# Full-array chunk products, paired chunk matrices and more block-product tiles in a hybrid attention and RWKV-7 block

## The chip, the core and the metric

The kernel runs on one core of a Trainium2 chip. The metric is the device time of one execution in microseconds. Times are the median of several executions; the profile is of one more execution of the same program.

## What is computed

A decoder block for 512 tokens of 1024 channels, all in float32. A normed input goes through one projection; its columns feed sparse attention (an indexer picks 128 keys per query) and an RWKV-7 recurrence of 8 heads of 64 channels. Both are gated, added, projected and added to the input. Then follows a gated feed-forward layer of 2816 hidden channels.

```python
# the recurrence, per token and head
def step(state, inp):
    r_t, d_t, k_t, v_t, kk_t, b_t = inp
    s_a = jnp.einsum('bhvk,bhk->bhv', state, -kk_t)
    state = state * d_t[:, :, None, :] + s_a[..., None] * b_t[:, :, None, :] \
        + v_t[..., None] * k_t[:, :, None, :]
    return state, jnp.einsum('bhvk,bhk->bhv', state, r_t)
...
h = h + merged @ w_out[l]
hn = _rms_norm(h, ffn_norm[l])
gate, up = _split(hn @ w_gate_up[l], (FFN_HIDDEN, FFN_HIDDEN))
h = h + (jax.nn.silu(gate) * up) @ w_down[l]
```

## The kernel before

**Order of the work.** TensorE's instructions run in the order in which the program emits them. The program is a set of generators (`Streams`, line 96) with ranks: `steps` 0, `inverses` and attention 1, `matrices` and `prepare` 2, norms 3, and the dense products (`products`) last, at 9. A generator yields a number of microseconds, or the name of a signal, and is resumed when that time has passed by a count of TensorE's work; meanwhile the next in rank is emitted. So dense products fill every gap of the recurrence. The instructions of the other engines are ordered when the program is built, by a simulation of their times, and then run in that fixed order on each engine.

**Dense products.** Weights come as chunks of 512 KB (`chunk`, line 232): loaded into `w_raw` (2 buffers), rounded by ScalarE into `w_hi`, the rest by GpSimd or VectorE into `w_lo` (3 buffers each). `dense_t` (line 255) runs three passes for each of eight blocks of 128 channels: high by high, high by low, low by high. PSUM has three tags: `d` and `c` with three banks, `i` with two.

**The recurrence** goes in 8 chunks of 64 tokens, two (`e` = 0, 1) in each of four tiles `t` of 128 tokens.
- `matrices` (line 754): for each chunk two groups `g` of heads (rows 0 to 63 and 64 to 127 of `KB` and `KR`), four products each into one `d` bank; VectorE masks the bank into `am[g]` (line 771) and adds the identity (line 775), ScalarE copies a part to `l16` (line 776). After each group the generator yields 0.5.
- `inverses` (line 781): triangular inverses by f16 products in the `i` banks.
- `chunk_values` (line 735): transposes the values of a tile and copies the halves to `ve[0:64]` and `vo[64:128]` (lines 740, 741); the other halves are filled later by the chunk's solution (line 898).
- `steps` (line 853), for each chunk: the first product of `am` with `vu` into `psz` (line 877); the product with the state, for which `KR` is the stationary side (line 881); the right side `B` (line 884); its product with the inverse (line 897) and `vu`'s other half (line 898); the state's growth (line 904) and the new state (lines 911 to 916); the last product of `am` with `vu` (line 920), which adds to `psz`, and the chunk's output `y` (line 921).

With `br` the half of the rows that the chunk's solution takes and `er` the other, a 64-row, 64-column operand puts a matmul into a quarter of the array, a 128-row, 64-column one into half of it:

```python
for h in range(H):
    cs = slice(h * 64, h * 64 + 64)
    r = br if h else slice(0, 128)
    mm(psz[r, cs], am[h % 2][er, h // 2, r], vu[er, cs], start=h == 0, stop=False, **go)
```

**Gate and up** (line 1135): 22 tiles of 128 hidden columns, for gate and up each. A plain tile is two `dense_t` of 24 passes over 512 tokens. The others take the 2x2 block scheme with 7 products: from the raw chunks `wg` and `wu` VectorE makes four sums `s1` to `s4` (lines 1149 to 1152), ScalarE and VectorE split seven 128x512 sides into high and low (lines 1155, 1156), TensorE runs `product` (line 1127) seven times, 12 passes of 256 tokens each, and VectorE adds the results (lines 1176, 1179, 1182, 1188, 1192) and multiplies (lines 1195, 1196); four banks are taken for each such tile. The token sides are made once (`seven_sides`, line 1221). From j = 2 on every third tile is plain. `wu` has three buffers (`fx`), the sums share eight (`uc`) with other tiles.

Of the kernel before, what the change touches and what calls it, by code (L numbers as in the profile page):

```python
# [82 lines left out]
for _n, _c in _PARS:  # L83
# [5 lines left out]
L = dict(norm=3.0, normed=1.3, score=0.6, pick=0.15, rms=9.0, sums=4.0, attn=(1.3, 1.1, 1.0, 1.0), attn_new=0.7, attn_out=2.0, sig=0.3,  # L89
         prep=5.0, oper=6.0, bonus=9.0, mat=0.5, mats=2.8, inv_u=4.2, inv_t=1.4, inv_r=1.4, inv_n=0.9, inv_e=1.8,  # L90
         inv=1.8, vals=0.6, st_b=1.0, st_u=1.36, st_m=1.4, hn_b=4.55, hn_n=6.55, hn_g=2.0)
# [36 lines left out]
def hybrid_block(ctx: ExitStack, tc: tile.TileContext, x, first, rows, consts, lora, rel_bias, stream, out):  # L128
    nc = tc.nc
# [9 lines left out]
    def bank(tag, dt=F32, name=None):  # L139
        n = {"d": 3, "i": 2, "c": 3}[tag]  # L140
        return pp.tile([128, 512], dt, name=name or "ps_" + tag, tag=tag, bufs=n)

    def unit(name, dt=F32):

        tag = "ua" if name in UA else "uc"
        return sp.tile([128, 512], dt, name=name, tag=tag, bufs=UNITS[tag])
# [14 lines left out]
    def mm(o, w, r, **kw):  # L161
        nc.tensor.matmul(o, w, r, **kw)  # L162
        n = 1
        for d in r.shape[1:]:
            n *= d
        st.now += max(n * 4 / 2400, 0.107) if r.dtype == F32 else max(n / 2400, 0.03)

    def flip(o, src, idn):
        nc.tensor.transpose(o, src, idn)  # L169
        st.now += 0.11  # L170
# [47 lines left out]
    def cst(name):  # L218
        o, e = CONST_AT[name]
        return con[:, o:e]  # L220
# [27 lines left out]
    def w_tile(n, eng=None):  # L248

        r = []  # L250
        for _ in range(n // 128):
            r += chunk(1024 // n, n, eng)
        return r
# [481 lines left out]
    def chunk_values(t):  # L735
        ps = bank("c")
        for p in range(4):
            flip(ps[:, p * 128:p * 128 + 128], zv[:, p, t * 128:t * 128 + 128], ident)
        ve, vo = unit("vu"), unit("vu")
        nc.scalar.activation(ve[0:64], ps[0:64], AF.Copy)  # L740
        nc.scalar.activation(vo[64:128], ps[64:128], AF.Copy)
        return ve, vo
# [11 lines left out]
    def matrices():  # L754
        yield "prep"
        for t in range(NT):
            if t > 1:
                yield f"inv{t - 2}"
                yield f"step{t - 2}"
            l16 = l16s[t % 2]  # L760
            for e in range(2):
                c = 2 * t + e
                am = [unit("am").rearrange("q (h t) -> q h t", h=4) for _ in range(2)]
                br = BLK[e]
                for g in range(2):
                    ps = bank("d").rearrange("q (h t) -> q h t", h=4)
                    for j in range(4):
                        o = g * 64
                        mm(ps[:, j], zz["KB"][j][o:o + 64, t, 2 * e:2 * e + 2], zz["KR"][j][o:o + 64, t, 2 * e:2 * e + 2],
                           start=True, stop=True)  # L770
                    nc.vector.tensor_mul(am[g], ps, cst("mask_a")[:, None, 64 - 64 * e:192 - 64 * e]
                                         .to_broadcast([128, 4, 128]))
                    hs = slice(g, H, 2)
                    lt = am[g][br, :, br]
                    nc.vector.tensor_add(lt, lt, ident[br, None, br].to_broadcast([64, 4, 64]))
                    nc.scalar.activation(l16[br, hs, br], lt, AF.Copy)
                    yield L["mat"]
                A[t, e] = am
            st.signal(f"mat{t}", L["mats"])

# [72 lines left out]
    def steps():  # L853
        M, M2 = None, mst[0]
        yield "zv"
        for t in range(NT):
            yield f"mat{t}"
            vus = chunk_values(t)
            y = unit("ytok")
            for e in range(2):  # L860
                c, vu, am = 2 * t + e, vus[e], A[t, e]

                br, er = BLK[e], BLK[1 - e]
                if c < 7:
                    kbs, kbt = unit("kbs"), unit("kbt")
                    p3 = lambda q: q.rearrange("q (p s) -> q p s", p=4)
                    nc.gpsimd.tensor_mul(p3(kbs), zz["KB_"][:, :, t, 2 * e:2 * e + 2].rearrange("q p a b -> q p (a b)"),
                                         PC[:, c, :, None].to_broadcast([128, 4, 128]))
                if e == 0:
                    yield L["vals"]  # L870
                psz = bank("c")

                go = dict(skip_group_check=True)
                for h in range(H):
                    cs = slice(h * 64, h * 64 + 64)
                    r = br if h else slice(0, 128)
                    mm(psz[r, cs], am[h % 2][er, h // 2, r], vu[er, cs], start=h == 0, stop=False, **go)
                if c:
                    yield f"state{c}"
                    for p in range(4):  # L880
                        mm(psz[:, p * 128:p * 128 + 128], zz["KR"][p][:, t, 2 * e:2 * e + 2], M[:, p], start=False,
                           stop=False, **go)
                B = unit("bmat")
                nc.vector.tensor_copy(B[br], psz[br])
                if c < 7:
                    pst = bank("c")
                    for p in range(4):
                        cs = slice(p * 128, p * 128 + 128)
                        flip(pst[:, cs], kbs[:, cs], ident)
                    nc.scalar.activation(kbt, pst, AF.Copy)  # L890
                if e == 0:
                    yield f"inv{t}"
                yield L["st_b"]
                psu = bank("c")
                for h in range(H):
                    cs = slice(h * 64, h * 64 + 64)
                    mm(psu[br, cs], U32s[t][br, cs], B[br, cs], start=True, stop=True)
                nc.vector.tensor_scalar(vu[br], psu[br], -1.0, None, op0=OP.mult)
                yield L["st_u"]
                if c < 7:  # L900
                    psg = bank("c")
                    for h in range(H):
                        p, o, cs = h // 2, (h % 2) * 64, slice(h * 64, h * 64 + 64)
                        mm(psg[o:o + 64, p * 64:p * 64 + 64], kbt[:, cs], vu[:, cs], start=True, stop=True)
                    g3 = psg[:, 0:256].rearrange("q (p v) -> q p v", p=4)
                    if c:
                        mp = bp.tile([128, 256], F32, name="mp", tag="mp", bufs=1).rearrange("q (p v) -> q p v", p=4)
                    for o in (0, 64):
                        q = slice(o, o + 64)
                        if c:  # L910
                            nc.gpsimd.tensor_mul(mp[q], M[q, :, q], PC[q, c, :, None].to_broadcast([64, 4, 64]))
                            nc.vector.tensor_add(M2[q, :, q], g3[q], mp[q])
                        else:
                            nc.vector.tensor_copy(M2[q, :, q], g3[q])
                    M, M2 = M2, mst[(c + 1) % 2]
                    st.signal(f"state{c + 1}", L["st_m"])
                for h in range(H):
                    cs = slice(h * 64, h * 64 + 64)
                    r = slice(0, 128) if h else br
                    mm(psz[er, cs], am[h % 2][r, h // 2, er], vu[r, cs], start=False, stop=h == 7, **go)  # L920
                nc.scalar.activation(y[er], psz[er], AF.Copy)
            st.signal(f"step{t}")
            st.add(3, head_norm(t, y))
# [64 lines left out]
    def products(wt, w2):  # L988
# [116 lines left out]
        def next_bank():  # L1105
            turn[0] += 1
            return bank(tags[(turn[0] - 1) % 8])

        def plain(j, ps, pu):
            g = unit("gsig")  # L1110
            nc.scalar.activation(g, ps, AF.Silu)
            nc.vector.tensor_mul(up_rows(j), pu, g)
# [20 lines left out]
                mm(ps, lo[:, ks], xh, start=False, stop=k == 3, skip_group_check=True)  # L1133

        for j in range(2, NF):
            if j % 3 == 2:
                ps, pu = next_bank(), next_bank()
                yield from dense_t(ps, w_tile(128, nc.vector), slice(0, 128), hn)
                yield from dense_t(pu, w_tile(128, nc.vector), slice(0, 128), hn)
                plain(j, ps, pu)  # L1140
                continue
# [56 lines left out]
        for g in range(2):  # L1198
            cs = slice(g * 512, g * 512 + 512)
            pss = [bank(tag) for tag in (("c", "c", "c", "i") if g == 0 else ("d", "d", "d", "i"))]  # L1200
            for k0 in range(0, NF, 2):
# [8 lines left out]
                for t, k in [(t, k) for t in range(NT) for k in range(2)] if last else [(t, k) for k in range(2)  # L1210
                                                                                   for t in range(NT)]:
                    j, ts = k0 + k, slice(t * 128, t * 128 + 128)
# [129 lines left out]
```

## Time and profile before

| | us |
|---|---|
| median of 3 executions | 909.22 |
| lowest, highest | 909.14, 909.89 |
| the profiled execution | 909.72 |
| its span, first to last instruction | 907.90 |
| outside the span | 1.82 |

The profile lists every instruction of the core with start and length. A matmul's length includes its latency, so rows overlap and the start of the next one tells what a pass costs. One f32 matmul of the program stands as two passes. The chunk stage lies from about 276 to 450 us of the span, gate and up from about 570 to 784.

### The profile page before, as it was taken

What the parts mean: (1) busy time and instruction counts of PE and PEld (TensorE: products, weight loads), DVE (VectorE), ACT (ScalarE), POOL (GpSimd) and SP (SyncE); (2) the same over time, 40 slices, a digit from 0 to 9 for tenths busy, and PEclk for the clock granted to TensorE, in tenths of its full rate; (3) what the DMA queues carried; (4) which work ended last, traced back from release to release, by engine and by line L of the source; (5) the groups of instructions that cost most, each with busy time, mean ns of one, the idle gap of its engine ahead of it and who ended that gap; (6) DMA issues with size and microseconds to landing.
All of it is one profiled execution on the core that took longest, in us unless ns stands there. A gap on an engine that the chain in (4) does not pass through costs nothing.

```text
span 907.9 us, 14949 instructions
## 1 busy us (share of the span) xinstructions
PE 891.5 (98%) x6018; PEld 775.3 (85%) x6018; DVE 572.6 (63%) x1064; ACT 394.0 (43%) x665; POOL 296.6 (33%) x216
## 2 busy tenths in 40 slices
PE   6999999999999999999999999999999999999998
PEld 5988898888687788887888998899999999988886
DVE  5279997786886457666435428777677667433433
ACT  5464586554643333334243234534344434434431
POOL 6477873221473444354146422000000000323321
PEclk9999999999999999999999999999999999999999
DMA  6331333111131210011433323232224132332431
GB/s 241 82 95 49 94 119 94 47 47 36 48 93 47 71 47 25 25 48 46 143 91 93 95 92 117 74 136 96 91 93 140 57 106 70 93 114 89 147 93 47
DMA packets 24182, 77.88 MB, mean 86 GB/s; under 512 B 2869, under 2 KB 4366, under 8 KB 24112
## 3 DMA queue, kind: packets, MB, share of 16 engines
q1 hardware_dynamic: 20688, 72.49, 25.6%
q10 hardware_dynamic: 3424, 4.43, 1.8%
q8 instruction: 47, 0.77, 0.3%
q14 instruction: 23, 0.19, 0.1%
HBM read 74.53 MB, written 2.38 MB: 85 GB/s over the span
## 4 chain that ended last, share of the span: by engine, by line
PE 84%; DVE 9%; POOL 2%; issue 2%; ACT 2%; DMA 1%; ACTq 0%; POOLq 0%; DVEq 0%
PE ps_d L162 48%; PE ps_c L162 19%; PE ps_i L162 14%; PE ps_c L169 2%; DVE score L447 2%; DVE max L446 2%; POOL w_lo L243 1%; DVE kr L716 1%; DVE sg L681 1%; DVE qs L470 1%; PE ps_i L169 0%; DVE score L427 0%; DMA grow<-in_rows_dram 0%; POOL bb L710 0%; POOL ag L719 0%
## 5 line engine op out<-in xcount | busy, mean ns | idle before, releaser
L243 POOL TENSOR_TENSOR w_lo<-w_raw,w_hi 128x1024 fp32r<-128x1024 f32 (+1 forms) x67 | 158.5, 2368 | 421.3 <-ACT w_hi L239 414.1
L239 ACT ACTIVATE w_hi<-w_raw 128x1024 fp32r<-128x1024 f32 x103 | 108.7, 1056 | 129.5 <-PE ps_d L162 93.9
L162 PE MATMUL ps_d<-xnl,w_hi 128*128 128x512 f32 (+2 forms) x360 | 141.4, 393 | 0.0
L162 PE MATMUL ps_d<-xnh,w_lo 128*128 128x512 f32 (+2 forms) x360 | 140.6, 390 | 0.4 <-POOL w_lo L243 0.4
L162 PE MATMUL ps_d<-xnh,w_hi 128*128 128x512 f32 (+2 forms) x360 | 140.7, 391 | 0.0
L162 PEld LDWEIGHTS ps_d<-xnh,w_lo 128*128 128x128 f32 x360 | 68.2, 189 | 12.2 <-issue 1.2
L162 PEld LDWEIGHTS ps_d<-xnl,w_hi 128*128 128x128 f32 x360 | 68.2, 190 | 11.8 <-issue 2.1
L162 PEld LDWEIGHTS ps_d<-xnh,w_hi 128*128 128x128 f32 x360 | 68.3, 190 | 10.7 <-issue 1.2
L1207 DVE TENSOR_TENSOR us<-u,us 128x512 fp32r<-128x512 f32 x44 | 36.7, 835 | 64.2 <-ACT us L1206 64.2
L243 DVE TENSOR_TENSOR w_lo<-w_raw,w_hi 128x1024 fp32r<-128x1024 f32 x38 | 49.2, 1296 | 18.9 <-ACT w_hi L239 18.3
L1206 ACT ACTIVATE us<-u 128x512 fp32r<-128x512 f32 x44 | 27.8, 632 | 67.4 <-PE ps_i L162 67.2
L162 PE MATMUL ps_d<-hnl,w_hi 128*128 128x256 f32 (+1 forms) x144 | 46.0, 319 | 0.4 <-DVE hnl L338 0.4
L162 PE MATMUL ps_d<-hnh,w_hi 128*128 128x256 f32 (+1 forms) x144 | 45.9, 319 | 0.0
L162 PE MATMUL ps_d<-hnh,w_lo 128*128 128x256 f32 (+1 forms) x144 | 45.9, 319 | 0.0
L162 PE MATMUL ps_c<-w_hi,us 128*128 128x512 f32 x132 | 44.1, 389 | 0.0
L162 PE MATMUL ps_d<-w_hi,us 128*128 128x512 f32 x132 | 44.1, 389 | 0.0
L1156 DVE TENSOR_TENSOR w_lo<-s,w_hi 128x512 fp32r<-128x512 f32 x39 | 26.1, 685 | 22.2 <-ACT w_hi L1155 22.2
L162 PE MATMUL ps_d<-w_hi,mh 128*128 128x256 f32 x120 | 34.0, 284 | 0.0
L162 PE MATMUL ps_d<-w_hi,ml 128*128 128x256 f32 x120 | 34.0, 283 | 0.0
L162 PE MATMUL ps_d<-w_lo,mh 128*128 128x256 f32 x120 | 34.0, 283 | 0.0
L162 PE MATMUL ps_i<-w_hi,us 128*128 128x512 f32 x88 | 33.9, 389 | 0.0
L584 ACT ACTIVATE lg<-lg,mx,qrs 128x128 f32<-128x128 f32 (+3 forms) x32 | 20.9, 652 | 24.9 <-DVE mx L583 24.9
(381 smaller groups left out, 2429.4 us busy)
## 6 DMA issues: line engine op xcount, KB each, us to landing
w_raw<-in_stream_dram SPq DMA_DIRECT2D x116, 512.0 KB, 3.5
wu_raw<-in_stream_dram SPq DMA_DIRECT2D x13, 512.0 KB, 4.3
xa<-in_x_dram SPq DMA_DIRECT2D x4, 512.0 KB, 5.8
ht<-in_x_dram ACTq DMA_DIRECT2D x8, 256.0 KB, 3.9
out_dram<-ht SPq DMA_DIRECT2D x8, 256.0 KB, 2.1
toep<-bias_table ACTq DMA_DIRECT2D x8, 128.0 KB, 3.5
gain<-in_rows_dram ACTq DMA_DIRECT2D x2, 256.0 KB, 4.1
con<-in_consts_dram SPq DMA_DIRECT2D x1, 321.0 KB, 7.0
```

The source lines that it names most:

```text
L162: nc.tensor.matmul(o, w, r, **kw)
L169: nc.tensor.transpose(o, src, idn)
L239: nc.scalar.activation(hi, raw, AF.Copy)
L243: eng.tensor_sub(lo[:, o:o + n_], raw[:, o:o + n_], hi[:, o:o + n_])
L446: nc.vector.max(m8, sc)
L447: nc.vector.match_replace(sc, m8, sc, TAKEN)
L470: nc.vector.scalar_tensor_tensor(lo[b, h], src[a], gain[a], hi[a, h], op0=OP.mult, op1=OP.subtract)
L584: nc.scalar.activation(lg, lg, AF.Exp, scale=scale, bias=mx[:, 2:3], accum_out=den[:, h:h + 1])
L681: nc.vector.tensor_tensor_scan(cum, seg, cum, 0.0, op0=OP.mult, op1=OP.add)
L1156: nc.vector.tensor_sub(l, w, h)
L1206: nc.scalar.activation(s[:, 0], up[k0 // 2][:, k], AF.Copy)
L1207: nc.vector.tensor_sub(s[:, 1], up[k0 // 2][:, k], s[:, 0])
```

## The change

Four places.
- `chunk_values`: two memsets by GpSimd zero the halves of `ve` and `vo` that are not yet filled, so that all 128 rows can be read.
- `steps`, first product: all heads use all 128 rows and give all 128 outputs. `steps`, last product: all heads use only the rows `br` and give the outputs `er`. What the last product added from the rows `er` now comes with the first.
- `matrices`: one yield of twice the time behind both groups, in place of one behind each.
- Gate and up: every sixth tile is plain in place of every third. Of j = 2 to 21 the plain ones were 2, 5, 8, 11, 14, 17 and 20 and are 2, 8, 14 and 20; 5, 11 and 17 are now block products.

```diff
--- before.py
+++ after.py
@@ -737,6 +737,9 @@
         ve, vo = unit("vu"), unit("vu")
+
+        nc.gpsimd.memset(ve[64:128], 0.0)
+        nc.gpsimd.memset(vo[0:64], 0.0)
         nc.scalar.activation(ve[0:64], ps[0:64], AF.Copy)
         nc.scalar.activation(vo[64:128], ps[64:128], AF.Copy)
         return ve, vo
@@ -774,7 +777,7 @@
                     nc.scalar.activation(l16[br, hs, br], lt, AF.Copy)
-                    yield L["mat"]
+                yield 2 * L["mat"]
                 A[t, e] = am
@@ -873,8 +876,7 @@
                     cs = slice(h * 64, h * 64 + 64)
-                    r = br if h else slice(0, 128)
-                    mm(psz[r, cs], am[h % 2][er, h // 2, r], vu[er, cs], start=h == 0, stop=False, **go)
+                    mm(psz[:, cs], am[h % 2][:, h // 2], vu[:, cs], start=h == 0, stop=False, **go)
@@ -916,8 +918,7 @@
                     cs = slice(h * 64, h * 64 + 64)
-                    r = slice(0, 128) if h else br
-                    mm(psz[er, cs], am[h % 2][r, h // 2, er], vu[r, cs], start=False, stop=h == 7, **go)
+                    mm(psz[er, cs], am[h % 2][br, h // 2, er], vu[br, cs], start=False, stop=h == 7, **go)
@@ -1133,7 +1134,7 @@
         for j in range(2, NF):
-            if j % 3 == 2:
+            if j % 6 == 2:
                 ps, pu = next_bank(), next_bank()
```

## Rows read from the trace of the kernel before

**Rows 1.** The page's engine table: busy us (share of the span), instructions.

```profile
PE 891.5 (98%) x6018; PEld 775.3 (85%) x6018; DVE 572.6 (63%) x1064; ACT 394.0 (43%) x665; POOL 296.6 (33%) x216
```

**Rows 2.** Waits of TensorE: engine, line, releaser: us in all, times, longest.

```profile
PE ps_c L162 <- DMA grow<-in_rows_dram: 5.0, 1, 5.0
PE ps_i L169 <- DVE xnl L338: 2.4, 3, 1.0
```

**Rows 3.** Tile `yr`: count, ns least/median/most, first and last start (us), shapes.

```profile
L162 PE MATMUL ps_d<-yr,w_hi x64: 389/389/389, 479.3 to 500.7; 128*128 128x512 f32 x64
...
L1059 DVE TENSOR_TENSOR yr<-zv,yr x4: 684/684/694, 469.0 to 470.8; 128x512 fp32r<-128x512 f32 x4
```

**Rows 4.** Timeline, TensorE: start (us), length (us), engine, line, operation, shapes, count [idle].

```profile
284.02 1.16 PE L162 MATMUL ps_d<-kr,kb 64*128 64x128 f32 x8
285.10 0.50 PE L162 MATMUL ps_d<-xnh,w_lo 128*128 128x512 f32 x1
...
286.00 1.16 PE L162 MATMUL ps_d<-kr,kb 64*128 64x128 f32 x8
```

**Rows 5.** Timeline, TensorE, from three stretches: attention, and two of a chunk.

```profile
206.67 1.00 PE L162 MATMUL ps_i<-vt,pt 128*128 128x64 f32 x8
...
321.49 1.14 PE L162 MATMUL ps_c<-bmat,u 64*64 64x64 f32 x16
322.57 0.50 PE L162 MATMUL ps_d<-xnh,w_lo 128*128 128x512 f32 x1
...
333.87 1.28 PE L162 MATMUL ps_c<-vu,am 64*64 64x64 f32 x16
```

**Rows 6.** Timeline, TensorE, from an even chunk's end into an odd one.

```profile
324.45 0.69 PE L162 MATMUL ps_c<-vu,kbt 128*64 128x64 f32 x16
325.06 2.60 PE L162 MATMUL ps_c<-vu,am 64*64 64x64 f32 x32
327.59 1.16 PE L162 MATMUL ps_c<-state,kr 128*128 128x128 f32 x8
328.59 0.60 PE L169 MATMUL ps_c<-fst,kbs 128*128 128x128 f32 x4
```

**Rows 7.** Timeline, TensorE, the start of an even chunk.

```profile
335.90 1.16 PE L162 MATMUL ps_d<-kr,kb 64*128 64x128 f32 x8
...
339.11 0.60 PE L169 MATMUL ps_c<-fst,kbs 128*128 128x128 f32 x4
```

**Rows 8.** GpSimd: a group (count, busy us, mean ns, idle); a row of the timeline.

```profile
L642 POOL MEMSET wa<- 64x512 f32 x2 | 1.0, 518 | 0.1
...
336.38 1.04 POOL L867 TENSOR_TENSOR kbs<-kb,pchunk 128x512 f32<-128x512 f32 x1
```

**Rows 9.** Groups of VectorE, 276 to 293 us: the reads of kr,kb's banks.

```profile
L771 DVE TENSOR_TENSOR am<-ps_d,con 128x512 f32<-128x512 f32 x8 | 5.5, 689 | 3.8 <-PE ps_d L162 3.7
```

**Rows 10.** Stretches of one gate-up tile: length, busy of each engine, clock, DMA.

```profile
607.34:618.25 10.91, 10.91 (x51) 9.02 (x49) 6.58 (x12) 3.42 (x6) 0.00 (x0) 1.00 0.14 45
...
628.32:638.40 10.08, 10.08 (x86) 10.08 (x85) 8.60 (x16) 4.75 (x8) 0.00 (x0) 1.00 0.55 162
```

**Rows 11.** Timeline, VectorE, around the start of a pair's second tile (628.32).

```profile
624.54 0.68 DVE L1149 TENSOR_TENSOR s<-wu_raw 128x512 f32<-128x512 f32 x1
...
627.42 0.68 DVE L1156 TENSOR_TENSOR w_lo<-s,w_hi 128x512 fp32r<-128x512 f32 x1
...
629.56 0.68 DVE L1156 TENSOR_TENSOR w_lo<-s,w_hi 128x512 fp32r<-128x512 f32 x1
630.16 0.42 DVE L1196 TENSOR_TENSOR u<-gsig,post 128x256 f32<-128x256 f32 x1
...
634.62 0.42 DVE L1182 TENSOR_TENSOR post<-ps_d,post 128x256 f32<-128x256 f32 x1
```

**Rows 12.** Timeline, TensorE, a wait late in the gate-up stage.

```profile
761.08 0.28 PE L162 MATMUL ps_c<-hnh,s4l 128*128 128x256 f32 x1
761.65 0.39 PE L162 MATMUL ps_d<-th,w_hi 128*128 128x256 f32 x1 [0.29 <-DVE post L1182]
```


## Prediction

> **What bounds the kernel now.** I read the engine table first, then the waits, then the timeline of the stages that the change touches. The engine table [rows 1] shows TensorE busy for 98% of the span, VectorE for 63%, GpSimd for 33%. The waits [rows 2] say that TensorE is hardly ever kept waiting: 5.0 us before the first matmul, 2.4 on the next line, and less on each of the eleven others. So the time is the sum of the start-to-start times of TensorE's passes, and a change is worth what it does to that sum, plus whatever new wait it makes. The chain of the chunks does not set the end either: its result `yr` is split by VectorE by about 471 us, and the first product that reads it starts at 479.3 [rows 3], with dense passes in between. A longer or shorter chunk is therefore priced in TensorE time alone, while those 8 us last.
>
> In the chunk stage a second cost is visible, the change of array shape. Eight 64x128 passes (kr,kb) and the three dense ones behind them go round in 1.98 us (284.02 to 286.00) [rows 4]. Without a switch it would be eight passes at 0.112 (below) and three dense passes at 0.227 (48 of them fill a plain tile's 10.91 us [rows 10]), 1.58 in all. So going into the shape and out again costs **0.40 us**, about 0.2 a switch.
>
> **Part A, the chunk's step.** It has two products. The *last* was one 64x64 head and seven 128x64 heads; now all eight are 64x64. The *first* was one 64x128 head and seven 64x64 heads; now all eight use the full array. An f32 matmul is two passes, so each product has 16.
> - Last product: 1.28 us long as a row, where the sixteen 64x64 passes of bmat,u are 1.14 [rows 5]. Gain 0.14 each; with its way out such a product takes 1.07 (321.49 to 322.57).
> - A full-array pass with 64 moving columns is in the trace as the attention's vt,pt: eight are 1.00 us long, some 0.27 of it the last one's latency, so 0.105 a pass [rows 5]. Eight passes of 128 columns (state,kr, 327.59 to 328.59) take 1.00, which with a switch's first load (0.10) leaves 0.112 [rows 6]. I take 0.112, against 0.058 for a 64x64 pass ((1.07 less 0.14 for the switch) / 16).
> - Odd chunk: last, first and state,kr run on end from 325.06 to 328.59 = 3.53 us [rows 6]. After: 1.07 + 0.10 entry + 24 x 0.112 = 3.86. **+0.33**, four times.
> - Even chunk with kr,kb right ahead: 335.90 to 339.11 = 3.21 [rows 7]; until now kr,kb and the first head share a shape. After, kr,kb must leave it (1.08, as in [rows 4]): 1.08 + 0.10 + 2.69 = 3.87. **+0.66**, in three tiles (the first has no state,kr, the rest is alike). In the last tile dense work is ahead, so two switches more fall away: 0.66 - 2 x 0.18 = +0.3.
> - The odd chunk's last product stands alone: -0.14, four times.
> Sum: 1.32 + 1.98 + 0.3 - 0.56 = **+3.0 us** on TensorE. Cross-check: 112 passes x 0.054 = 6.0 dearer, 22 switches fewer at 0.14 = 3.1 cheaper. Bounds +2.0 (switches at 0.18) to +3.6 (at 0.11).
>
> The drains show in the rows as the 0.15 to 0.2 us a switch above; kbt, whose passes change the column half each time but not the shape, gets sixteen into 0.69 us [rows 6], so a changed place alone costs nothing. The Trainium skill, TensorEngine Tiling (Array Packing), § Tiling Modes, says the same (changing the mode drains TensorE, changing the tile does not), and the trace agrees with it by those numbers. But § Performance Considerations of the same page advises row and column tiling where a dimension is 64 or less, which speaks against the full array here; what that would make of the time is the second rival.
>
> The zero halves of `vu` are eight memsets on GpSimd. The same form costs 0.52 us there [rows 8]. GpSimd is idle two thirds of the time, and a memset waits for no data, only for its buffer; I cost them at **0**, hidden in the time between the buffer's release and the tile's start. If that cover is gone, one stands behind kbs (336.38 to 337.42) [rows 8], and the first product, with all of TensorE's queue behind it (dense passes too), starts at 337.9 in place of 336.9: 1.0 us in each of four tiles, +4 at most.
>
> **Part B, matrices.** The two groups of eight kr,kb passes follow each other with no return to other work; sixteen groups become eight pairs, so eight times 0.40 goes: **-3.2 us**. If going from rows 0 to 63 to rows 64 to 127 cost as much as one switch, it would be -1.6; the nearest row is kbt, so I take -3.2. What it adds: a pair holds two of the three `d` banks, and the next pair or dense tile waits until VectorE has read one (0.69 us [rows 9]). The next pair comes 1 us of dense passes later, which covers one read. Bounds 0 to 8 x 0.69 = +5.5; the waits of TensorE for VectorE's reads are small everywhere [rows 2], so I take half a read in all, **+0.3**.
>
> **Part C, gate and up.** A plain tile takes 10.91 us, a tile of seven block products behind another such 10.08 [rows 10]. Three plain tiles (j = 5, 11, 17) change: 3 x 0.83 = **-2.5 us**. Each lies between two pairs, so there are now three runs of five. VectorE's work for such a tile: eleven operations of 512 columns that start 0.60 apart (629.56, 630.16) and seven of 256 of 0.42 each [rows 11], 9.5 us. That is below 10.07, so it keeps up. The second tile of a pair is the pattern for the rest: its sums start at 624.54, the first low part is there at 628.10, and the second product wants it near 630.0 (12 passes of 0.12 and two more after the tile's start at 628.32), 1.9 us to spare. A third tile's sums then find VectorE free behind the add of 634.62, so at 635.0, which is 0.4 later in their tile: 1.5 to spare, and the same again for the fourth and fifth. Bounds: -2.5, and what the slower rival takes.
>
> **Sum.** 3.0 - 3.2 + 0.3 - 2.5 = -2.4 us. The profiled execution took 909.72 (span 907.90 and 1.82 around it); the median is 909.22, 0.5 less. On the median that gives **906.8 us**, on the profiled execution 907.3.
>
> **The rivals.**
> - *The gain is eaten by small waits (no change).* The memset behind kbs (up to +4), a pair short of a bank (up to +5.5), or B at -1.6. Two of them at a quarter of their bounds give +2.2: 909.0. For it: TensorE works in order, and three things now hold it that did not. Against: the two largest lines of the waits name neither GpSimd nor am, and the others are smaller. 24%.
> - *The small tiles were right (no change).* Half of each gap that I count as a switch is latency that the next pass pays anyway; the full passes then buy little for their 6.0. With switches at half, A is +4.5 and B -1.6, the sum +0.7: 909.9. Against: the gaps are between starts of passes, and the round of [rows 4] holds 0.40 that no pass explains. This is how it would go by the advice of the Trainium skill's page above, TensorEngine Tiling (Array Packing), § Performance Considerations. 4%.
> - *VectorE's queue holds TensorE in the runs of five (slower).* The place is the third add of a tile (L1182): the seventh product writes on in the bank that it reads. In the tile of 628.32 it runs at 634.62, 6.3 us in; it must be done 8.6 us in (six products of 1.44). Once it was not: late in the stage the seventh product starts 0.57 us behind the pass before it in place of 0.12 [rows 12]. If each tile that follows another (twelve in three runs) pays these 0.45, that is +5.4: 912.2. It decides when VectorE has over 2 us of other work queued ahead of that add. Against: 9.5 us of work in 10.07. For: its queue has a fixed order and is now full of such work for 50 us on end. 11%.
> - *A gets no dearer,* because the full passes overlap their loads as kbt's passes do: 3.0 less, 903.8. Against: vt,pt is that very form. 3%.
>
> **How the numbers follow.** The forecast has the remaining 58%, with its own range 905.2 to 908.0. Below 905.2 lie the last rival and a little of the forecast; upward the range goes to 910.8, which takes in the small waits and leaves out the slower rival. A measurement here can tell about 0.2% (1.8 us) from no change, so 907.4 and 911.0 are the borders. Most of the forecast lies under the first: faster 0.57, same 0.32, slower 0.11.
>
> **What would show it.** Steps: the first product as 16 full-array passes of 0.112, no 64x128 or 128x64 row of vu,am left. Matrices: kr,kb in groups of sixteen, 1.98 us from start to the next dense pass. Gate and up: tiles of 10.07 us in fives. A first product that waits for GpSimd's vu, or a `ps_d` pass that waits for am, would show the first rival; a wait for post (L1182) the third. The forecast is wrong at its root if a full-array pass is far from 0.112 us or a switch far from 0.15 to 0.2.

## The result and the profile after

| | before | after |
|---|---|---|
| median, us | 909.18 (6 executions) | 903.80 (6 executions) |
| lowest, highest | 908.86, 909.89 | 903.37, 905.28 |
| the profiled execution | 909.72 | 903.37 |
| its span | 907.9 | 901.5 |

The ratio is 0.9943, with an interval of 0.9933 to 0.9954: **5.4 us faster**, where 2.4 was forecast. The time lies 1.4 us below the low end of the range. One of the experiments below has a number that needs a word here: the kernel with the pairs alone took 906.5 to 907.8 us in seven executions and 910.1 to 911.5 in five, whose granted clock over the span was 0.994 to 0.996 in place of 0.999 to 1.0.

As before, the engine table of the page after comes first (busy us, share, instructions; for [rows 1]), then its waits of TensorE (for [rows 2]).

```profile
PE 886.4 (98%) x6126; PEld 779.5 (86%) x6126; DVE 584.5 (65%) x1109; ACT 399.6 (44%) x686; POOL 304.4 (34%) x224
```

```profile
PE ps_c L162 <- DMA grow<-in_rows_dram: 4.7, 1, 4.7
PE ps_i L169 <- DVE xnl L338: 2.4, 3, 1.0
```

TensorE is 98% busy, and the list has no new wait of any size. So the difference is again in its passes, and a split by stages finds it. The marks are the first starts in the views by tile: `kr` (first matrices), `yr` (first product behind the chunks). First of the kernel before (tile, count, ns least/median/most, first to last start in us, shapes):

```profile
L162 PE MATMUL ps_d<-kr,kb x128: 272/272/373, 276.1 to 385.0; 64*128 64x128 f32 x128
```

and of the kernel after:

```profile
L162 PE MATMUL ps_d<-kr,kb x128: 272/272/373, 274.6 to 382.3; 64*128 64x128 f32 x128
...
L162 PE MATMUL ps_d<-yr,w_hi x64: 389/389/389, 476.0 to 497.3; 128*128 128x512 f32 x64
```

With [rows 3] the chunk stage took 479.3 - 276.1 = 203.2 and takes 476.0 - 274.6 = 201.4: 1.8 us less, where the forecast's terms for it (A and B) came to +0.1. Gate and up, from the first pass with `hnh` (the normed tokens) to the first with `us` (the gated product that the last projection reads), went from 234.7 to 231.7: 3.0 less, where 2.5 was forecast. The remaining 1.5 of these two profiles lie ahead of 276 us, where TensorE's order of instructions is the same in all the kernels of the table below. In their traces, one execution each, that stretch ends between 274.6 and 276.1, so I take most of it for a difference between executions. (The medians differ by 5.4, the two spans by 6.4.)

Two stretches of the timeline of TensorE after, a pair of matrices (for [rows 4]) and an even and an odd chunk (for [rows 7, 6]; in the odd one last and first product stand in one row, the first's passes are the later sixteen):

```profile
274.57 1.71 PE L162 MATMUL ps_d<-kr,kb 64*128 64x128 f32 x16
276.21 0.50 PE L162 MATMUL ps_d<-xnh,w_lo 128*128 128x512 f32 x1
...
280.63 2.16 PE L162 MATMUL ps_d<-kr,kb 64*128 64x128 f32 x16
282.72 0.50 PE L162 MATMUL ps_d<-xnh,w_hi 128*128 128x512 f32 x1
...
284.08 2.32 PE L162 MATMUL ps_d<-kr,kb 64*128 64x128 f32 x16
286.33 0.44 PE L169 MATMUL ps_c<-fst,zv 128*128 128x128 f32 x2
...
336.40 2.00 PE L162 MATMUL ps_c<-vu,am 128*128 128x64 f32 x16
338.24 1.11 PE L162 MATMUL ps_c<-state,kr 128*128 128x128 f32 x8
...
364.37 3.07 PE L162 MATMUL ps_c<-vu,am 64*64 64x64 f32 x32
367.27 1.11 PE L162 MATMUL ps_c<-state,kr 128*128 128x128 f32 x8
368.22 0.60 PE L169 MATMUL ps_c<-fst,kbs 128*128 128x128 f32 x4
```

The step is as forecast: sixteen full passes go round in 1.84 (336.40 to 338.24), 0.115 each, and an odd chunk's last, first and state product in 3.85 (364.37 to 368.22; forecast 3.86). The pair is not: **1.64 us** (274.57 to 276.21) in place of 1.98. Six of the eight pairs take 1.64; the third and the fourth take 2.09 and 2.25. The list of waits shows nothing of these two, since the pass before still has latency to run when the late one starts.

Gate and up after, two tiles of seven products in the middle of a run of five and the plain tile behind (for [rows 10]; the view is of stretches: length, busy of each engine, clock, DMA):

```profile
604.00:614.08 10.08, 10.08 (x87) 10.08 (x85) 9.22 (x19) 4.89 (x10) 0.00 (x0) 1.00 0.32 104
614.08:624.16 10.08, 10.08 (x87) 10.08 (x85) 9.22 (x19) 4.89 (x10) 0.00 (x0) 1.00 0.31 106
...
634.24:645.15 10.91, 10.91 (x51) 9.02 (x50) 6.79 (x12) 3.54 (x7) 0.00 (x0) 1.00 0.16 48
```

VectorE (the third busy time) is at 9.22 of 10.08 us, and TensorE loses nothing. The third add in the tile of 604.00, in VectorE's timeline, with the idle time before it:

```profile
609.96 0.42 DVE L1183 TENSOR_TENSOR post<-ps_d,post 128x256 f32<-128x256 f32 x1 [0.29 <-PE ps_d L162]
```

VectorE has waited 0.29 us for TensorE there, not TensorE for VectorE.

### The profile page after: what moved, and what is told of

The parts are those of the page before. It is cut to its first block, busy times and chain, and to the rows that moved or that the text cites. A ratio compares the mean times of both kernels' runs of the same rounds, so it can differ in the third digit from the quotient of the medians.

```text
span 901.5 us, 15252 instructions
## 1 busy us (share of the span) xinstructions
PE 886.4 (98%) x6126; PEld 779.5 (86%) x6126; DVE 584.5 (65%) x1109; ACT 399.6 (44%) x686; POOL 304.4 (34%) x224
## 4 chain that ended last, share of the span: by engine, by line
PE 84%; DVE 9%; POOL 2%; issue 2%; ACT 1%; DMA 0%; ACTq 0%; POOLq 0%; DVEq 0%
PE ps_d L162 47%; PE ps_c L162 20%; PE ps_i L162 14%; DVE score L447 2%; PE ps_c L169 2%; DVE max L446 2%; POOL w_lo L243 1%; DVE kr L716 1%; DVE sg L681 1%; DVE am L774 1%; DVE am L778 1%; DVE qs L470 1%; DVE score L427 0%; PE ps_i L169 0%; POOL bb L710 0%
## 5 line engine op out<-in xcount | busy, mean ns | idle before, releaser
L239 ACT ACTIVATE w_hi<-w_raw 128x1024 fp32r<-128x1024 f32 x97 | 102.4, 1056 | 120.5 <-PE ps_d L162 99.8
L243 DVE TENSOR_TENSOR w_lo<-w_raw,w_hi 128x1024 fp32r<-128x1024 f32 x32 | 42.1, 1316 | 18.8 <-ACT w_hi L239 18.4
L1157 DVE TENSOR_TENSOR w_lo<-s,w_hi 128x512 fp32r<-128x512 f32 x48 | 32.5, 685 | 12.2 <-ACT w_hi L1156 12.2
L1156 ACT ACTIVATE w_hi<-w_raw 128x512 fp32r<-128x512 f32 x32 | 20.2, 633 | 29.3 <-PE ps_c L162 12.1
```

What stands on the lines that cost most here:

```text
L239: nc.scalar.activation(hi, raw, AF.Copy)
L243: eng.tensor_sub(lo[:, o:o + n_], raw[:, o:o + n_], hi[:, o:o + n_])
L1156: nc.scalar.activation(h, w, AF.Copy)
L1157: nc.vector.tensor_sub(l, w, h)
```

## The experiments

All kernels side by side. The stages are of each kernel's profiled execution, cut at the marks above before rounding; a time is the median on the chip, a ratio that to the kernel before on the same chip, with its interval.

| kernel | us | ratio | first kr,kb at | chunk stage | gate and up |
|---|---|---|---|---|---|
| before | 909.2 | | 276.1 | 203.3 | 234.7 |
| after | 903.8 | 0.9943 (0.9933 to 0.9954) | 274.6 | 201.4 | 231.7 |
| step alone | 911.8 | 1.0033 (1.0021 to 1.0045) | 274.7 | 206.0 | 234.9 |
| pairs alone | 907.8 | 0.9995 (0.9983 to 1.0007) | 275.3 | 200.7 | 234.7 |
| more sevens alone | 906.1 | 0.9971 (0.9961 to 0.9982) | 275.4 | 203.3 | 231.7 |
| pairs of the same rows | 905.8 | 0.9967 (0.9955 to 0.9979) | 275.2 | 203.2 | 231.7 |
| pairs dealt in turn | 901.4 | 0.9918 (0.9904 to 0.9932) | 274.6 | 199.3 | 231.6 |
| pairs spread | 906.6 | 0.9973 (0.9962 to 0.9984) | 275.4 | 203.8 | 231.7 |
| first product by quarters | 902.7 | 0.9929 (0.9915 to 0.9943) | 275.7 | 200.7 | 231.7 |
| no plain tile | 904.5 | 0.9950 (0.9937 to 0.9963) | 274.9 | 201.4 | 231.3 |
| pairs alone, with zeros | 904.7 | 0.9946 (0.9934 to 0.9959) | 275.6 | 199.1 | 234.8 |
| three edits | 898.5 | 0.9876 (0.9860 to 0.9892) | 274.6 | 196.7 | 229.6 |
| three edits, spread | 898.1 | 0.9873 (0.9856 to 0.9890) | 275.4 | 198.4 | 229.6 |
| three edits, spread, state later | 897.2 | 0.9864 (0.9849 to 0.9879) | 274.7 | 196.9 | 229.6 |

**The three parts, each alone.** The question was which term had the error. The step: the memsets and the two products of the diff, on the kernel before.

> The chunk's step alone (full-array first product, equal 64x64 last product, zeroed halves of vu); matrices and gate-up as in the kernel before. Theory (part A was priced right, part B wrongly): +3.0 us against the kernel before, 912.2 (bounds +2.0 to +3.6). Rival (part A is cheaper than its sum, and that is where the 3 us come from): 909.2 or less. In the trace: a first product of 16 passes in about 1.83 us, an odd chunk's last, first and state,kr in about 3.86, and kr,kb groups of eight in 1.98 to the next dense pass but one run.

Measured 911.8, +2.5 us; the chunk stage of its trace is 2.7 longer. kr,kb go in eights as before, the first product takes 1.84, and an odd chunk 3.85. Part A was priced rightly, a little high.

More block products: only the edit of `j % 3`.

> Three more tiles of gate and up by seven products alone. Theory: 3 x 0.83 = -2.5, and -3.0 if the pause of 0.45 us late in the stage of the kernel before goes as well: 906.2 to 906.7. Rival (VectorE's add holds TensorE within the runs of five tiles): up to 912.

Measured 906.1, -3.1; the stage is 3.0 shorter and nothing else moves. The 0.5 us above three times 0.83 is the pause of [rows 12], which is in neither trace with the new order of tiles.

The pairs: only the yield.

> The paired matrices alone; the step and gate-up as in the kernel before. Theory 1 (the two groups lie in different row halves of the array and overlap where they meet): a pair takes 1.64 us to the next pass; 8 x 0.40 for the switches, 8 x 0.34 for the overlap and about +1.1 for two waits for a bank: -4.8, so 904.4. The prediction's price (1.98 a pair, no overlap): -3.2 and +1.1, 907.1.

Measured 907.8, and 906.6 for the profiled execution: close to the prediction's price, but by luck. By its trace the first two pairs take 1.64 as theory 1 wants; the bank waits are larger than in the kernel after, and the fourth pair takes 3.25 in place of 2.25. So the parts don't simply add up: alone they give +2.5, -3.1 and -1.4, -2.0 in all, and together -5.4. Two things had to be told apart, the price of a pair and what the other parts do to its wait.

**Why a pair is cheap.** The two groups of a pair lie in different row halves of the array. The rival is that the shape alone, kept for sixteen passes, is enough. In the next kernel both groups of a pair read the same rows (first both chunks' even heads, then both chunks' odd heads); TensorE's order of shapes stays that of the kernel after, and the two groups still write two banks (... stands for lines left out).

```diff
-            for e in range(2):
-                ...
-                for g in range(2):
+            for g in range(2):
+                for e in range(2):
                     ...
                 yield 2 * L["mat"]
```

> The changed kernel, with the partners of a pair of matrices exchanged: both groups of a pair now read the same half of the rows (head parity the same, the two chunks of a tile in turn); the order of shapes is unchanged. Theory 1 (it is the different row halves that overlap): 1.98 us for a pair in place of 1.64, +0.34 each, +2.7 in all less what the waits for a bank take up: about 906 against 903.8. Theory 2 (the pair is cheap because the array keeps its shape for sixteen passes, whatever the rows): 1.64 as before, 903.8.

Its first pair, in the timeline of TensorE:

```profile
275.23 2.05 PE L162 MATMUL ps_d<-kr,kb 64*128 64x128 f32 x16
277.21 0.50 PE L162 MATMUL ps_d<-xnh,w_lo 128*128 128x512 f32 x1
```

With the same rows a pair takes **1.98** us (275.23 to 277.21), to the hundredth what was forecast for all pairs, and the kernel 905.8. The eight pairs take 16.0 us, against 14.2 in the kernel after; that is the 1.8 by which the chunk stage is longer. So the price of a switch was right, and what was missed is an overlap of the two row halves. Theory 1 then says more: deal the passes of the two groups out in turn, and they overlap throughout.

```diff
+                pp2 = [bank("d").rearrange("q (h t) -> q h t", h=4) for _ in range(2)]
+                for j in range(4):
+                    for g in range(2):
+                        o = g * 64
+                        mm(pp2[g][:, j], zz["KB"][j][o:o + 64, t, 2 * e:2 * e + 2], ...)
...
```

> The changed kernel with the passes of a pair dealt out in turn: one head of the upper row half, one of the lower, and so on. Theory 1 (passes in different row halves overlap wherever they are next to each other, not only at the seam): sixteen passes at half of 0.112 and the 0.40 of the way in and out, about 1.2 to 1.3 us a pair in place of 1.64; -0.35 to -0.45 eight times, -2.8 to -3.6, less some 1 us if the waits for a bank grow: 901 to 902.5 against 903.8. Theory 2 (the seam saves once, by what lies in the queue there): 1.64, 903.8; if each change of the row half costs time, more than 1.98.

```profile
274.62 1.16 PE L162 MATMUL ps_d<-kr,kb 64*128 64x128 f32 x16
275.72 0.50 PE L162 MATMUL ps_d<-xnh,w_lo 128*128 128x512 f32 x1
```

Dealt in turn (the same view), a pair takes **1.09** us (274.62 to 275.72), and the kernel 901.4. Four of the eight pairs do; the third and fourth, with a wait for VectorE's read of a bank, take 1.67 and 1.68, and behind two more the next pass comes 0.4 late. Single passes, which the view merges into one row, start 0.105 to 0.112 apart within a row half in these traces, and 0.004 to 0.007 behind a pass of the other half. In the kernel after this happens only at the seam, where the first three passes of the second group run beside the last ones of the first: three times 0.112, the 0.34 that the forecast lacked. The Trainium skill, TensorE: Matmul & The Clock Gate, Part 3: Packing small matmuls — row/col tiling, has this rule: matmuls whose operands lie in different groups of rows run at the same time, with starts some 4 ns apart. The traces agree, at 4 to 7 ns; the forecast had drawn only on what a change of shape or of place costs.

**What holds the pairs, and what the zeros do.** In the kernel with the pairs alone, VectorE's rows around the fourth pair (L771 reads a bank, L775 is the add that stands between two reads; with the memsets these lines lie three further down), GpSimd's rows, and TensorE's. GpSimd's `kbs` is a product that the chunk's transposes read.

```profile
283.22 0.67 DVE L771 TENSOR_TENSOR am<-ps_d,con 128x512 f32<-128x512 f32 x1
283.82 0.67 DVE L790 TENSOR_TENSOR uu<-l,lev 128x1024 f16<-128x1024 f16 x1
284.52 1.78 DVE L775 TENSOR_TENSOR am<-am,fst 64x256 f32<-64x256 f32 x1
286.34 0.69 DVE L771 TENSOR_TENSOR am<-ps_d,con 128x512 f32<-128x512 f32 x1
...
283.82 1.20 POOL L801 TENSOR_TENSOR l16b<-am,l 64x256 f16<-64x256 f32 x1 [0.81 <-ACT l L776]
284.99 1.03 POOL L867 TENSOR_TENSOR kbs<-kb,pchunk 128x512 f32<-128x512 f32 x1
...
284.92 1.16 PE L162 MATMUL ps_d<-kr,kb 64*128 64x128 f32 x8
287.09 1.16 PE L162 MATMUL ps_d<-kr,kb 64*128 64x128 f32 x8 [1.01 <-DVE am L771]
```

The add takes 1.78 where others of its form take 0.42 with GpSimd idle, and ends 0.28 us after GpSimd's `kbs`; the read behind it comes late, and TensorE stands 1.01 us. In the kernel after, `kbs` of the first chunk runs at 270.97, ahead of the matrices, and so it does with the step alone (271.06), which has the memsets and no pairs: the program's fixed order on GpSimd came out otherwise with the memsets in it. To see whether that is the cause, the next kernel has the pairs and the memsets, with the products of the kernel before, which don't read the zeros.

```diff
         ve, vo = unit("vu"), unit("vu")
+        nc.gpsimd.memset(ve[64:128], 0.0)
+        nc.gpsimd.memset(vo[0:64], 0.0)
```

> The paired matrices alone, and with them the eight memsets of vu's unused halves; the step's products and gate-up as in the kernel before, so that the zeros serve nothing. Theory (the pairs alone gained little because GpSimd's kbs product of the first chunk ran amid the matrices and held VectorE's add of am for 1.36 us, and so the bank of the fourth pair; the memsets move kbs ahead of the matrices in GpSimd's order): kbs starts near 271 us in place of 285.0, the add of am takes 0.8 us at most in place of 1.78, the fourth pair about 2.25 in place of 3.25, the later second pairs 1.64 in place of 2.02; -1.9 against the pairs alone, about 904.7. Rival (the long waits come from the order of the step, not from GpSimd): the pairs as in the kernel with pairs alone, 906.6 to 907.8.

Its rows of GpSimd, VectorE and TensorE for the same place:

```profile
271.98 1.04 POOL L870 TENSOR_TENSOR kbs<-kb,pchunk 128x512 f32<-128x512 f32 x1
...
284.73 0.79 DVE L778 TENSOR_TENSOR am<-am,fst 64x256 f32<-64x256 f32 x1
...
285.13 2.31 PE L162 MATMUL ps_d<-kr,kb 64*128 64x128 f32 x16
287.38 0.66 PE L169 MATMUL ps_c<-fst,zv 128*128 128x128 f32 x4
```

`kbs` is at 271.98, the add at 0.79, the fourth pair at 2.25, the kernel at 904.7: as the theory said, but for the later second pairs, which went only from 2.02 to 1.99. So eight memsets that nobody reads are worth 1.6 us of chunk stage, by what they do to another engine's order. With the memsets in step and pairs alike the parts nearly add up: +2.5, -3.1 and -4.5 are -5.1, where -5.4 was measured. The Trainium skill, SBUF — State Buffer, Summary: rules for kernel authors, has this as well: it says that of a VectorE operation with two inputs in SBUF and a GpSimd operation that reads SBUF the second waits until the first is done. The rows agree in that the add ends 0.28 us after GpSimd's product; why `kbs`, which starts 0.47 us after the add, goes ahead of it they don't show. There is one more such add in the kernel after, and it too ends 0.28 us after GpSimd's product (VectorE, then GpSimd). It may be what delays the third pair there; no run tests that.

```profile
277.67 1.83 DVE L778 TENSOR_TENSOR am<-am,fst 64x256 f32<-64x256 f32 x1
...
276.85 2.37 POOL L243 TENSOR_TENSOR w_lo<-w_raw,w_hi 128x1024 fp32r<-128x1024 f32 x1 [2.50 <-issue]
```

**Can the waits be taken away?** The due time of the next pair three times as far (`yield 6 * L["mat"]`).

> The changed kernel with more dense work between two pairs of matrices (the due time of the next pair three times as far). Theory: the two long pairs (2.09 and 2.25 us) are waits for a bank that VectorE has not read, so all eight take 1.64: -1.06, about 902.8, if nothing behind them comes late. Rival (the long pairs are something else, or the wait moves to another tile): 903.8.

All eight pairs take 1.64, so the long ones were waits for a bank. But the kernel is slower than the one after, 906.6, and its chunk stage 2.4 longer. The likely reason is that the dense passes spent there are missing later. TensorE's waits in the chunk stage, a list that is empty in the kernel after, come to 2.7:

```profile
PE ps_i L162 <- DVE rr L819: 1.6, 1, 1.6
PE ps_i L162 <- ACT tt L824: 0.4, 1, 0.4
PE ps_d L169 <- POOL bv L943: 0.4, 1, 0.4
PE ps_c L162 <- ACT vu L743: 0.3, 1, 0.3
```

**Does the same hold for columns?** The first product by 64x64 quarters in place of full passes, for each head first one column half and then the other; the memsets left out, since all that is read is there.

```diff
-                    mm(psz[:, cs], am[h % 2][:, h // 2], vu[:, cs], start=h == 0, stop=False, **go)
+                    for r in (br, er):
+                        mm(psz[r, cs], am[h % 2][er, h // 2, r], vu[er, cs], start=h == 0, stop=False, **go)
```

> The changed kernel with the chunk's first product by 64x64 quarters, the two column halves in turn, 32 passes in place of 16 full ones; no zeroed halves of vu are needed. Theory 1 carried from rows to columns (a pass next to one of another column half overlaps with it; kbt's passes go round in 0.69/16 = 0.043 us): 32 x 0.043 = 1.4 at most in place of 1.79, and one switch less beside the last product, which has the same shape: -0.5 to -0.8 in each of eight chunks, -4 to -6, 898 to 900. Rival (64x64 passes take the 0.058 of the last product whatever their neighbours, as the prediction held): 32 x 0.058 = 1.86, less a switch, 0 to -1: 903 to 904.

The product, and then the second group of the fourth pair (timeline of TensorE), and the stretches of that wait and behind the pair (the clock is the third number from the end):

```profile
337.70 1.15 PE L162 MATMUL ps_c<-vu,am 64*64 64x64 f32 x32
338.78 1.16 PE L162 MATMUL ps_c<-state,kr 128*128 128x128 f32 x8
...
287.43 1.40 PE L162 MATMUL ps_d<-kr,kb 64*128 64x128 f32 x8 [0.99 <-DVE am L771]
```

```profile
286.43:287.43 1.00, 0.01 (x1) 0.00 (x0) 0.94 (x3) 0.41 (x1) 0.00 (x0) 1.00 0.00 0
288.76:289.52 0.76, 0.76 (x5) 0.76 (x5) 0.76 (x2) 0.42 (x1) 0.00 (x0) 0.50 0.00 0
289.52:291.08 1.56, 1.56 (x5) 0.81 (x3) 0.51 (x2) 1.15 (x2) 0.00 (x0) 0.50 0.00 0
```

Thirty-two quarter passes take **1.08** us (337.70 to 338.78), 0.034 each, where sixteen full ones take 1.84 and sixteen of one and the same quarter 1.07. Theory 1 holds for columns too. The kernel gained only 1.1 us of it, 902.7: without the memsets `kbs` is back amid the matrices, and the fourth pair takes 3.47. In the profiled execution, at 903.7, the granted clock was 0.50, the 1.2 GHz level, for over 2 us behind the wait of 0.99 us, so its chunk stage in the table is longer by that too.

**Runs of seven-product tiles without a plain one.** `if False:` in place of `j % 6 == 2`.

> The changed kernel with every tile of gate and up from j = 2 on by seven products, so that no plain tile gives VectorE time to catch up. If VectorE keeps up (its 9.5 us of work in 10.08): 0.83 less for each plain tile that goes, 16.6 us for twenty such tiles at most and 0.83 times their count; the stretch of gate-up then is 0.120 us a pass throughout. Rival (VectorE's queue holds TensorE in long runs, the prediction's slower rival): a pause of 0.4 us or more at the add of the third product in each later tile.

The stage is 231.3, 0.4 less than after, where four tiles at 0.83 are 3.3; on the chip, 904.5, the kernel can't be told from the one after. The pauses are at the head of the first tile (timeline of TensorE), and one of 0.3 at the end:

```profile
575.07 0.39 PE L162 MATMUL ps_i<-th,w_hi 128*128 128x256 f32 x1 [0.17 <-ACT w_hi L1156]
575.29 0.28 PE L162 MATMUL ps_i<-tl,w_hi 128*128 128x256 f32 x1
577.39 0.39 PE L162 MATMUL ps_i<-th,w_lo 128*128 128x256 f32 x1 [1.82 <-DVE w_lo L1157]
```

Behind them nineteen tiles run on end without a pause of 0.25 us but that last one: VectorE doesn't fall behind. What the first plain tile is good for is its start: with j = 2 alone plain, in the kernels below, the stage is 229.6 and the 1.82 us are not there.

**The edits together.** Pairs dealt in turn, quarters with the memsets kept, and only j = 2 plain; then with one and a half times the dense work between the pairs of the first two tiles (`3 * L["mat"]` for t < 2), and then with the state's due time 0.6 later (`st_m=2.0`).

> The changed kernel with three edits together: passes of a pair dealt out in turn by row half, the first product by 64x64 quarters in turn by column half (the memsets stay), and only the tile j = 2 of gate and up plain. By their sums: 901.4 with the pairs in turn; eight first products at 0.75 to 0.9 less, -6 to -7; three tiles at 0.83 less, -2.5; about 892 if no wait grows, 895 if the waits for a bank and for the state take 1.5 us each.

> The kernel with the three edits together, and half as much dense work again between two pairs of the first two tiles. Theory: the third and fourth pair no longer wait for a bank: -1 us against the three edits alone. Rival (the dense work is missing later, as when the due time was three times as far): no gain or slower.

> The kernel with the three edits and the spread pairs, and the state's product due 0.6 us later. Theory: with the quarters an odd chunk's state,kr comes too early by some 0.45 us (1.51 in place of 1.08 in two chunks with the quarters alone), and dense work put ahead of it hides that: -0.9 to -1.3. Rival (the wait moves to the next link of the chunk's chain): no gain.

898.5, 898.1 and 897.2; the last has a ratio of 0.9864 (0.9849 to 0.9879), and all three beat both kernels. Of the last two steps neither can be told from nothing by these intervals. The expected 892 to 895 was missed in the chunk stage. In the first of the three kernels (timeline of TensorE):

```profile
335.50 1.16 PE L162 MATMUL ps_d<-kr,kb 64*128 64x128 f32 x16
337.70 0.39 PE L162 MATMUL ps_i<-tt,l 128*128 128x64 f16 x8 [1.04 <-ACT tt L826]
```

The pass behind the pair belongs to the inverse, whose chain through ScalarE and VectorE isn't shorter than before, and TensorE now reaches it 1.04 us too early; the same stands behind the second pair of the last tile. Spread, the third and fourth pair are at 1.09 as expected, but a wait for `rr`, a tile of the inverse, of 1.9 us comes instead. In its profiled execution the granted clock was 0.50 from the end of that wait on, for over 2 us, so its 198.4 is not to be set against 196.7. And the theory of the last edit was wrong: state,kr still goes round in 1.51 in two chunks, since the transposes behind it wait for GpSimd's `kbs`.

## Why the prediction was wrong

The sign was right, and so were the reasons for A and C. The size was not, since B left an overlap out; the mark that the forecast set for the matrices, 1.98 us for a group of sixteen, came out at 1.64.
- **Part A held.** +3.0 forecast, +2.5 alone on the chip, full passes at 0.115 (forecast 0.112). Neither rival about it came true: the full passes didn't get cheap, and the switches were not half as dear; a pair of the same rows costs 1.98 as [rows 4] made it.
- **Part B is the step that failed**, at "if going from rows 0 to 63 to rows 64 to 127 cost as much as one switch, it would be -1.6; the nearest row is kbt, so I take -3.2". Both ends took the change of the row half as a cost or as nothing. It is a gain: 0.34 us a pair, -2.7 for eight, shown by the pairs of the same rows, which take 1.98 where the others take 1.64 (the kernels 905.8 and 903.8, the chunk stages 203.2 and 201.4). kbt was the right row but read too narrowly: its sixteen passes take 0.61 us to the next product [rows 6], where the sixteen of bmat,u, all in one quarter, take 1.07 [rows 5]. In the trace of before kbt's single passes start in twos, 6 to 7 ns apart, so the overlap of two halves could be read there. The forecast took from it only that a changed place costs nothing; a bound below nothing was missing on that term.
- **The bank waits of B were real**, the small waits of the first rival: two pairs of 2.09 and 2.25 are +1.06, where +0.3 was forecast. Of this 0.68 is the overlap, which both lose: their second group starts 0.13 and 0.28 us behind the last pass of the first, in the other pairs 0.33 before it; the waiting itself is the other 0.38. In the pairs of the same rows, which have no overlap to lose, the same two are 2.01 and 2.13, 0.18 over 1.98. With these the two corrections of B come to -2.7 + 0.8 = -1.9, which is the chunk stage's difference from the forecast (-1.8 for +0.1).
- **The memsets at nothing held, for a wrong reason.** The forecast looked for them behind `kbs`, where they could only cost. They stand ahead of it, and with them `kbs` of an even chunk runs some six us earlier in the stage (328.61, 54.0 behind the first matrices; before, 336.38 [rows 8], 60.3 behind them) and that of the first leaves the matrices. Without it the pairs would have lost 1.6 us of their gain. No view of before shows how the fixed order of an engine comes out after an instruction is added.
- **Part C was mis-sized by 0.5.** Three tiles at 0.83 were right (runs of five at 10.08), and the pause of [rows 12] went with the old order. The forecast used that row only as the price of the slower rival. That rival did not come: VectorE's third add runs 6.0 us into a tile (609.96) and VectorE has waited for TensorE before it; even nineteen tiles on end don't bring it.

So of the 3.0 us by which the forecast missed, 1.9 are B and 0.5 are C by the traces. The other 0.6 is not settled. By the medians of the parts alone (the pairs with zeros for B), A came 0.5 under its price, B 1.6 and C 0.6, 2.7 in all; but each of these medians has an interval some 2 us wide, and the stretch ahead of 276 us differs by up to 1.5 between executions.

## What to carry to other kernels

Price small matmuls by their neighbours: passes next to each other in different halves of the array overlapped here, so ones that share a half should be dealt out in turn with those of the other; this was worth 0.55 us a pair where no wait took it back, and full-array passes with zeros were the dearer way. A term that rests on "a changed place" needs a bound on both sides of nothing. And when an instruction is added to an engine whose order a program plans, look at what it moves: an add on VectorE with two inputs from SBUF took 1.78 us in place of 0.42 beside a GpSimd product of 1.03, so the place of such a product can be worth more than its length.

## What was not expected of the hardware

- Passes in different row halves start 4 to 7 ns apart and sixteen of them take 1.09 us dealt in turn, 1.64 in two groups, 1.98 in one half. Thirty-two 64x64 passes that change the column half go round in 0.034 us each, sixteen in one quarter in 0.067.
- A VectorE add of 64x256 that takes 0.42 us took 1.78 beside a GpSimd product of 1.03, and 1.83 beside one of 2.37.
- A wait of 0.99 us was followed by a granted clock of 0.50 for over 2 us in one kernel, while one of 1.01 us at the same place in the profiled execution of another left it at 1.00. Behind a wait of 1.90 us for `rr` it fell to 0.50 with the three edits spread, and behind one of 1.87 at the same place with the state later it did not. Why is open.
